# The ends of the FFN blocks of a one-layer encoder step: another order of loads, weights and normalization

## The chip, the cores and the metric

The kernel runs on one core of one Trainium2 chip. The metric is the device time of one execution in microseconds (us), lower is better. The core has the engines PE (TensorE, matrix products), DVE (VectorE), ACT (ScalarE), POOL (GpSimd) and SP (SyncE, which here issues DMAs). A tile framework takes the operations as the program writes them, gives them buffers ("slots" of named tags) and semaphores, and may put instructions of one engine into another order than written.

## What is computed

One layer for 2176 tokens (17 tiles of 128). A mixer (attention, delta rule, state space model) comes first and is not touched. Then:

```python
x = layer_norm(DN_ALPHA * x + mix, lp['ln1_g'], lp['ln1_b'])
hid = jnp.square(jax.nn.relu(x @ lp['w_up'] + lp['b_up']))            # 1024 -> 4096
x = layer_norm(DN_ALPHA * x + hid @ lp['w_down'], lp['ln2_g'], lp['ln2_b'])   # 4096 -> 1024
```

`layer_norm` takes mean and variance over the 1024 features of a token, divides by the square root of variance + 1e-5, multiplies by g and adds b.

## The kernel before

Every matrix product is made of three: each operand is split into a rounded high part (an ACT cast to fp32r) and the rest (a subtraction, on DVE or POOL), and `mm3` sums high x high, low x high and high x low in PSUM. Rows of PE with L68, L69, L70 are these three.

The FFN (from about 1436 us on) goes over three blocks of tokens, 6, 6 and 5 tiles (`BLOCKS`), and in a block over 16 chunks `c` of 256 of the 4096 hidden features. For one chunk there is first the up product, in a Strassen-like form with seven products instead of eight: `f_up1` makes four (operands B11, T2, T3, T1) and `f_up2` three (B21, T4, B22). `f_up_raw` loads the chunk's weights (tile `wur`, two DMAs of 512 KB), `f_up_weights` makes seven combinations and splits them: seven ACT casts and eleven POOL operations of 128x512 into seven slots `wu`. `f_up2` ends with relu, square and the split of the result into `hh` and `hl` (`f_h`). Then the down product: `f_down_weights` loads two halves (`wdr`, three slots) and splits them into `wdh`, `wdl` (two slots each); `f_down` goes tile by tile, half by half of the 1024 outputs, with 2 x 3 matmuls each (12 for a tile, four PSUM slots `fdp`), and a DVE sum adds each result to `fy`, which holds y of the block's tiles (L1583 in chunk 0, L1585 otherwise).

In the steady state PE's order is: three products of `f_up2(c)`, four of `f_up1(c+1)`, then `f_down(c)`; the weights are made one chunk ahead.

At the end of blocks 0 and 1 three things meet. The next block's x must be loaded and transformed (`f_load`, per tile: a load into a `wdr` slot, eight PE transposes into PSUM tiles `ftps`, two ACT copies into `fxs`, four POOL subtractions, seven ACT casts and seven DVE subtractions): it is written between the tiles of `f_down(14)`, as only then the operands `fx...` of the block are free. The hidden part of chunk 15, whose `f_up2` is written with the argument `down`, is split only behind `f_down(14)`. And y of each tile is normalized as soon as it is summed up (`layer_norm` on DVE, `norm`, `later`), stored to the output `o_y`, and only then its `fy` slot can take the next block's x. Chunk 0 of the next block needs its weights again, which `f_up_raw(0)` and `f_up_weights` make anew.

In the last block the products of chunks 14 and 15 are summed in one `f_down`, and each tile is normalized after its sums: four tiles with ACT and POOL (`light`), the last with DVE.

SP issues all DMAs in one queue in program order, and a DMA that waits for a slot holds up what is behind it. Places that the prediction names: `f_load` L1406 to L1437, `f_down` L1569 to L1586, `norm` and `later` L1601 to L1607, the block ends L1639 to L1658, `layer_norm` L1296 to L1317, `rsqrt` L349 to L351.

Of the kernel before, what the change touches and what calls it, by code (L numbers as in the profile page):

```python
# [39 lines left out]

LOADS = 5
LATE = 1


class K:
# [31 lines left out]
    def run(self, upto=99):  # L77
        nc, A = self.nc, self.A
        with self.es:
# [22 lines left out]
            self.x1 = d.tile([NT, DM], F32, name="x1")  # L102
            self.ident = self.ld(self.cst, "c_ident")
# [1192 lines left out]
    def layer_norm(self, pool, y, g, b, tag, light=None):  # L1296


        nc = self.nc
        V = nc.vector  # L1300
        bs = pool.tile([128, 2, nc.vector.BN_STATS_DIM], F32, name=tag + "bs", tag=tag + "bs")
        for i in range(2):
            V.bn_stats(bs[:, i], y[:, i * 512:(i + 1) * 512])
        mv = pool.tile([128, nc.vector.BN_AGGR_DIM], F32, name=tag + "mv", tag=tag + "mv")
        V.bn_aggr(mv, bs)
        ve = pool.tile([128, 1], F32, name=tag + "ve", tag=tag + "ve")
        V.tensor_scalar(ve, mv[:, 1:2], 1e-5, None, OP.add)
        rn = self.rsqrt(pool, ve, 1, tag)
        if light:
            nm = pool.tile([128, 1], F32, name=tag + "nm", tag=tag + "nm")  # L1310
            V.scalar_tensor_tensor(nm, mv[:, 0:1], -1.0, rn, OP.mult, OP.mult)
            nc.scalar.activation(y, y, AF.Identity, scale=rn, bias=nm)
            light.tensor_tensor(y, y, g, OP.mult)
            light.tensor_tensor(y, y, b, OP.add)
            return
        V.scalar_tensor_tensor(y, y, mv[:, 0:1], g, OP.subtract, OP.mult)
        V.scalar_tensor_tensor(y, y, rn, b, OP.mult, OP.add)  # L1317
# [21 lines left out]
    def w_out(self, es):  # L1339
# [9 lines left out]
        for t in range(1, NTILE + 1):  # L1349
# [7 lines left out]
            if t in (6, 8, 10, 12, 14, 16):  # L1357
                self.f_load(0, t // 2 - 3, self.fx0, rp, "mr", 2)
# [26 lines left out]
    def w_norm(self, t, y, pool, g, b):  # L1385
        y = y.rearrange("p k t -> p (k t)")
        self.layer_norm(pool, y, g, b, "l1")
        self.nc.sync.dma_start(self.x1[t * 128:(t + 1) * 128], y)
# [15 lines left out]
    def f_load(self, t0, i, ops, pool, tag, bufs):  # L1404


        nc = self.nc
        x = pool.tile([128, DM], F32, name="fxr", tag=tag, bufs=bufs)
        nc.sync.dma_start(x, self.x1[(t0 + i) * 128:(t0 + i + 1) * 128])
        xs = [self.fx.tile([128, 4, 128], F32, name="fxs", tag=f"fxs{j}") for j in range(2)]  # L1410
# [8 lines left out]
        c1, c2 = (self.fx.tile([128, 4, 64], F32, name=n, tag=n) for n in ("fxc1", "fxc2"))  # L1419
        P = nc.gpsimd  # L1420

        def split(o, src):
            ts = slice(i * 64, i * 64 + 64)
            self.split(ops[o][0][:, :, ts], ops[o][1][:, :, ts], src)

        split("B11", b["B11"])
        P.tensor_tensor(c1, b["B12"], b["B11"], OP.subtract)  # L1427
        P.tensor_tensor(c2, b["B22"], c1, OP.subtract)
        split("T2", c2)
        P.tensor_tensor(b["B12"], b["B22"], b["B12"], OP.subtract)  # L1430
        split("T3", b["B12"])
        split("T1", c1)
        split("B21", b["B21"])
        P.tensor_tensor(c2, b["B21"], c2, OP.subtract)
        split("T4", c2)
        split("B22", b["B22"])
# [69 lines left out]
    def f_up2(self, s, h, down=None):  # L1506
# [5 lines left out]
        def relu2(r, i, src):  # L1512
# [3 lines left out]
        def keep(r, i, q):  # L1516
# [4 lines left out]

        def done(r, i, q, src):
            relu2(r, i, src)
            keep(r, i, q)
# [7 lines left out]
        if down:  # L1532
            for ps, o in (("x", "B21"), ("z", "T4"), ("v", "B22")):
                self.f_product(s, ps, o, False)
            relu2(c22, 1, c22)
            c21, c12 = add("z"), add("v")
            relu2(u, 0, s["x"])
            relu2(c21, 1, c21)
            relu2(c12, 0, c12)
            down()  # L1540
            keep(u, 0, 0)
            keep(c12, 0, 1)
            keep(c21, 1, 0)
            keep(c22, 1, 1)
            return
# [23 lines left out]
    def f_down(self, c, h, wd, ys):  # L1569
# [5 lines left out]
        for i, y in enumerate(ys):  # L1575
            ts = slice(i * 128, (i + 1) * 128)
            for z in range(2):
                zs = slice(z * 512, (z + 1) * 512)
                ps = self.fdp.tile([128, 512], F32, name="fdp", tag="fd")
                for k in range(m):  # L1580
                    self.mm3(ps, h[k][0][:, ts], h[k][1][:, ts], wd[k][0][:, zs], wd[k][1][:, zs], k == 0, k == m - 1)
                if c == 0:
                    V.scalar_tensor_tensor(y[:, zs], y[:, zs], ALPHA, ps, OP.mult, OP.add)  # L1583
                else:
                    V.tensor_tensor(y[:, zs], y[:, zs], ps, OP.add)  # L1585
            yield i  # L1586

    def ffn(self, es):
# [10 lines left out]
        norms = []  # L1599

        def norm(t, y, light):  # L1601
            self.layer_norm(self.fe, y, *rows, "l2", light)
            nc.sync.dma_start(A["o_y"][t * 128:(t + 1) * 128], y)

        def later(n):
            for _ in range(min(n, len(norms))):
                norm(*norms.pop(0))  # L1607

        def run(steps):
            for _ in steps:  # L1610
                pass

        for bi, (t0, nt) in enumerate(BLOCKS):
# [3 lines left out]
            for c in range(NC):  # L1617
                if bi + c == 0:
                    w = self.wu0
# [3 lines left out]
                later(2)  # L1623
                if c:
                    wd = self.f_down_weights(c - 1)
                if c < NC - 1:
                    if c:
                        run(self.f_down(c - 1, h, wd, ys))
                    h = self.f_h(nt)
                    self.f_up2(s, h)  # L1630
                    later(2)
# [7 lines left out]
            h15 = self.f_h(nt) if not last else None  # L1639
            if not last:  # L1640
                t1, n1 = BLOCKS[bi + 1]

                def down():
                    nonlocal ops
                    ops = self.f_x(n1)
                    for i in self.f_down(NC - 2, h, wd, ys):
                        if i < LOADS:
                            self.f_load(t1, i, ops, self.fw, "wdr", 3)

                self.f_up2(s, h15, down)  # L1650
                wd = self.f_down_weights(NC - 1)
                w = self.f_up_weights(self.f_up_raw(0))
                for i in self.f_down(NC - 1, h15, wd, ys):
                    if i + LOADS < n1:
                        self.f_load(t1, i + LOADS, ops, self.fw, "wdr", 3)
                    norms.append((t0 + i, ys[i], nc.vector))
                    if i >= LATE:
                        later(1)  # L1658
            else:
# [7 lines left out]
                for i in self.f_down(NC - 2, h + h15, wd, ys):  # L1667
                    norm(t0 + i, ys[i], nc.gpsimd if i < nt - 1 else None)
# [117 lines left out]
```

## Time and profile before

| | |
|---|---|
| time, median of 3 runs (lowest, highest) | 2952.27 us (2949.34, 2952.82) |
| the profiled execution: time, span | 2949.45 us, 2947.7 us |
| mean granted TensorE clock of it | 0.981 |
| PE busy | 2803.6 us, 95% of the span |
| DVE, ACT, POOL busy | 1996.0, 1324.7, 930.5 us (68, 45, 32%) |
| chain that ended last | PE 71%, DVE 15%, DMA 4%, ACT 3%, issue 3%, POOL 3% |

Busy time is the time in which an engine executes; the span is the time from the first to the last instruction of the profiled execution. The chain is followed back from the last instruction to what released it each time, so its shares tell which engine was the last to be waited for. The shares are means over very different stages; for a change at certain places the rows of these places count.

### The profile page before, as it was taken

What the parts mean: (1) busy time and instruction counts of PE and PEld (TensorE: products, weight loads), DVE (VectorE), ACT (ScalarE), POOL (GpSimd) and SP (SyncE); (2) the same over time, 40 slices, a digit from 0 to 9 for tenths busy, and PEclk for the clock granted to TensorE, in tenths of its full rate; (3) what the DMA queues carried; (4) which work ended last, traced back from release to release, by engine and by line L of the source; (5) the groups of instructions that cost most, each with busy time, mean ns of one, the idle gap of its engine ahead of it and who ended that gap; (6) DMA issues with size and microseconds to landing.
All of it is one profiled execution on the core that took longest, in us unless ns stands there. A gap on an engine that the chain in (4) does not pass through costs nothing.

```text
span 2947.7 us, 46191 instructions
## 1 busy us (share of the span) xinstructions
PE 2803.6 (95%) x16677; PEld 2451.0 (83%) x16677; DVE 1996.0 (68%) x5093; ACT 1324.7 (45%) x2735; POOL 930.5 (32%) x842
## 2 busy tenths in 40 slices
PE   8999999989999999999999999988999998899996
PEld 8988888867777777788889899967999897799996
DVE  7588887797655778778755555497555557855557
ACT  3554544342456666612334344453334345444442
POOL 0011111231100000002554544554544445555653
PEclk9999999989999999999999999999999999999998
DMA  5634454464557441144512122133112122422221
GB/s 183 199 106 127 108 138 112 131 174 122 179 195 224 141 129 51 58 168 165 185 66 86 57 67 77 58 118 122 61 63 81 58 72 95 144 76 73 86 86 43
DMA packets 282923, 330.37 MB, mean 112 GB/s; under 512 B 84530, under 2 KB 217478, under 8 KB 282374
## 3 DMA queue, kind: packets, MB, share of 16 engines
q1 hardware_dynamic: 282694, 327.42, 35.5%
q8 instruction: 131, 2.15, 0.3%
q14 instruction: 98, 0.80, 0.1%
HBM read 265.04 MB, written 64.93 MB: 112 GB/s over the span
## 4 chain that ended last, share of the span: by engine, by line
PE 71%; DVE 15%; DMA 4%; ACT 3%; issue 3%; POOL 3%; SPq 0%; ACTq 0%; POOLq 0%; DVEq 0%
PE fdp L68 7%; PE fdp L69 7%; PE fdp L70 7%; PE pps L69 3%; PE pps L70 3%; PE pps L68 3%; PE aob L1220 2%; PE fupx L69 2%; PE fupx L68 2%; PE fupx L70 2%; PE wops L69 2%; PE wops L68 2%; PE wops L70 2%; PE fupz L70 2%; PE fupz L68 2%
## 5 line engine op out<-in xcount | busy, mean ns | idle before, releaser
L1459 POOL TENSOR_TENSOR wu<-wur,wu 128x512 fp32r<-128x512 f32 x329 | 444.5, 1356 | 683.1 <-ACT wu L1458 672.7
L1585 DVE TENSOR_TENSOR fy<-fy,fdp 128x512 f32<-128x512 f32 x500 | 342.3, 687 | 306.2 <-PE fdp L70 306.0
L68 PE MATMUL fdp<-wdh,hh 128*128 128x512 f32 x1068 | 419.8, 395 | 21.6 <-DVE fy L1583 12.2
L70 PE MATMUL fdp<-wdh,hl 128*128 128x512 f32 x1068 | 418.1, 392 | 1.1 <-DVE hl L1520 1.1
L69 PE MATMUL fdp<-wdl,hh 128*128 128x512 f32 x1068 | 418.7, 392 | 0.0
L1458 ACT CAST wu<-wur 128x512 fp32r<-128x512 f32 x329 | 202.9, 619 | 421.3 <-DMA wur<-in_w_upL 165.1
L68 PE MATMUL pps<-xh,wh 128*128 128x384 f32 (+2 forms) x800 | 280.5, 352 | 9.0 <-ACT xh L63 8.6
L69 PE MATMUL pps<-xl,wh 128*128 128x384 f32 (+2 forms) x800 | 279.5, 350 | 2.9 <-DVE xl L64 2.8
L70 PE MATMUL pps<-xh,wl 128*128 128x384 f32 (+2 forms) x800 | 277.5, 347 | 0.5 <-DVE wl L64 0.3
L68 PEld LDWEIGHTS fdp<-wdh,hh 128*128 128x128 f32 x1068 | 202.2, 190 | 66.0 <-DVE fy L1583 13.8
L70 PEld LDWEIGHTS fdp<-wdh,hl 128*128 128x128 f32 x1068 | 202.1, 189 | 44.3 <-DVE hl L1520 1.9
L69 PEld LDWEIGHTS fdp<-wdl,hh 128*128 128x128 f32 x1068 | 202.1, 189 | 40.2
L63 ACT CAST wdh<-wdr 128x1024 fp32r<-128x1024 f32 x94 | 98.1, 1049 | 262.9 <-PE fdp L70 262.9
L1520 DVE TENSOR_TENSOR hl<-fre,hh 128x384 fp32r<-128x384 f32 (+1 forms) x186 | 137.7, 743 | 71.5 <-ACT hh L1519 71.5
L68 PEld LDWEIGHTS pps<-xh,wh 128*128 128x128 f32 x800 | 152.2, 191 | 19.7 <-ACT xh L63 9.1
L69 PEld LDWEIGHTS pps<-xl,wh 128*128 128x128 f32 x800 | 152.2, 190 | 14.3 <-DVE xl L64 5.4
L70 PEld LDWEIGHTS pps<-xh,wl 128*128 128x128 f32 x800 | 151.9, 190 | 11.3 <-issue 1.8
L64 DVE TENSOR_TENSOR wl<-wr,wh 128x512 fp32r<-128x512 f32 (+1 forms) x152 | 105.3, 699 | 61.1 <-ACT wh L63 57.9
L63 ACT CAST wh<-wr 128x512 fp32r<-128x512 f32 (+1 forms) x152 | 92.8, 619 | 78.2 <-DMA wr<-in_w_inA 39.7
L64 DVE TENSOR_TENSOR wdl<-wdr,wdh 128x1024 fp32r<-128x1024 f32 x94 | 116.1, 1237 | 3.1 <-ACT wdh L63 3.1
L1427 POOL TENSOR_TENSOR fxc<-fxs 128x256 f32<-128x256 f32 x17 | 20.8, 1223 | 294.8 <-ACT fxs L1417 288.8
L1189 ACT ACTIVATE P<-P,st 128x640 f32<-128x640 f32 (+4 forms) x128 | 97.2, 761 | 35.5 <-DVE st L1186 35.3
(555 smaller groups left out, 7289.9 us busy)
## 6 DMA issues: line engine op xcount, KB each, us to landing
wur<-in_w_upL SPq DMA_DIRECT2D x96, 512.0 KB
wdr<-in_w_dnL SPq DMA_DIRECT2D x96, 512.0 KB
wr<-in_w_inA SPq DMA_DIRECT2D x70, 512.0 KB
TU<-tD SPq DMA_DIRECT2D x34, 256.0 KB
y<-in_x SPq DMA_DIRECT2D x17, 512.0 KB
x<-y SPq DMA_DIRECT2D x17, 512.0 KB
fxr<-x SPq DMA_DIRECT2D x17, 512.0 KB
fy<-x SPq DMA_DIRECT2D x17, 512.0 KB
```

The lines of the kernel that those rows point to most:

```text
L63: nc.scalar.copy(hi, src)
L64: nc.vector.tensor_tensor(lo, src, hi.bitcast(F32), OP.subtract)
L68: mm(out, lh, rh, start=first, stop=False, **kw)
L69: mm(out, lh, rl, start=False, stop=False, **kw)
L70: mm(out, ll, rh, start=False, stop=last, **kw)
L1189: nc.scalar.activation(x, x, AF.Exp, scale=-1.0, bias=st[:, q:q + 1], accum_out=st[:, 2 + q:3 + q])
L1220: mm(ob[q * 64:q * 64 + 64, p], vt[j][:, h * 64:(h + 1) * 64], PT[:, k], start=j == 0, stop=j == nk - 1)
L1427: P.tensor_tensor(c1, b["B12"], b["B11"], OP.subtract)
L1458: self.nc.scalar.copy(hi, src)
L1459: P.tensor_tensor(lo, src, hi.bitcast(F32), OP.subtract)
L1520: V.tensor_tensor(hl, r, hh.bitcast(F32), OP.subtract)
L1585: V.tensor_tensor(y[:, zs], y[:, zs], ps, OP.add)
```

## The change

The values computed are the same. There are five parts:

1. `f_load` becomes a generator with three steps: the DMA; the transposes, copies, POOL subtractions and casts to the high parts; the low parts (five on DVE, two on POOL). At a block end `step(k)` after tile k of `f_down(14)` and `f_down(15)` starts the next load at k = 0, 1, 3, 5, 7, 9.
2. The last two tiles of `f_down(14)` and the first two of `f_down(15)` are made as a pair, with the half of the weights as the outer loop and four PSUM tiles at a time. The hidden part of chunk 15 lies in four of the seven `wu` slots, and `f_up2` is the usual one.
3. The weights of chunk 0 are stored to DRAM (`wu0D`, seven DMAs of 512 KB) at the start of the FFN and read back at the block ends, three while `f_down(15)` runs and four behind it.
4. y of blocks 0 and 1 goes unnormalized to DRAM (`x2`) and is normalized in the next block, one tile in every second chunk (`norm_left`): loaded behind `f_up1` of an odd chunk, and in the next chunk its statistics after tile 0 of `f_down`, the square root after tile 1, the product with ACT and POOL after tile 2.
5. `layer_norm` works in halves of 512 columns, and `rsqrt1` makes the inverse root of ten TENSOR_SCALAR operations, on 128x1. In the last block three tiles go by ACT and POOL and two by DVE, and the last tile is stored in halves.

```diff
-LOADS = 5
-LATE = 1
+LOADS = (0, 1, 3, 5, 7, 9)
...
+    def rsqrt1(self, pool, var, eps, tag, pin):
...
+        pin(V.tensor_scalar(x, var, eps, None, OP.add))
+        y = y.bitcast(I32)
+        V.tensor_scalar(y, x.bitcast(I32), 1, None, OP.logical_shift_right)
+        V.tensor_scalar(y, y, -1.0, float(0x5f3759df), OP.mult, OP.add)
+        V.tensor_scalar(xh, x, -0.5, None, OP.mult)
+        cur = y.bitcast(F32)
+        for _ in range(3):
+            V.tensor_scalar(s, cur, cur, xh, OP.mult, OP.mult)
+            V.tensor_scalar(z, s, 1.5, cur, OP.add, OP.mult)
+            cur = z
+        return z
...
+        for o in ("B11", "B21", "B22", "T1", "T2", "T4", "T3"):
+            nc.scalar.copy(self.f_part(ops, o, 0, i), b[o])
+        yield
+        for o in ("B11", "B21", "B22", "T1", "T2", "T4", "T3"):
+            e = P if o in ("B21", "B22") else nc.vector
+            e.tensor_tensor(self.f_part(ops, o, 1, i), b[o], self.f_part(ops, o, 0, i).bitcast(F32), OP.subtract)
...
+    def f_up_again(self, i):
+
+        w = self.fw.tile([128, 2, 4, 128], F32R, name="wu", tag="wu", bufs=7)
+        self.nc.sync.dma_start(w.rearrange("p a b c -> p (a b c)").bitcast(F32), self.wu0D[i])
+        return w
...
+            todo = [(i + j, z) for j in range(2 if i == pair else 1) for z in range(2)]
...
+            for x, k in [(x, k) for k in range(m) for x in todo] if ps else [(x, k) for x in todo for k in range(m)]:
...
+        def norm_left():
+            t = left.pop(0)
+            ts = slice(t * 128, (t + 1) * 128)
+            y = [self.fx.tile([128, 512], F32, name="fyn", tag=f"fxs{j}") for j in range(2)]
+            for j in range(2):
+                nc.sync.dma_start(y[j], self.x2[ts, j * 512:j * 512 + 512])
+            yield
+            yield from self.layer_norm(self.fe, y, *rows, "l2", nc.gpsimd,
...
-                self.f_up2(s, h15, down)
+                self.f_up2(s, h15)
+                ops = self.f_x(n1)
+                loads = [self.f_load(t1, i, ops, self.fw, "wdr", 3) for i in range(n1)]
...
+                for i in self.f_down(NC - 2, h, wd, ys, nt - 2):
+                    step(i)
                 wd = self.f_down_weights(NC - 1)
-                w = self.f_up_weights(self.f_up_raw(0))
-                for i in self.f_down(NC - 1, h15, wd, ys):
-                    if i + LOADS < n1:
-                        self.f_load(t1, i + LOADS, ops, self.fw, "wdr", 3)
-                    norms.append((t0 + i, ys[i], nc.vector))
-                    if i >= LATE:
-                        later(1)
+                w = []
+                for i in self.f_down(NC - 1, h15, wd, ys, 0):
+                    t = t0 + i
+                    nc.sync.dma_start(self.x2[t * 128:(t + 1) * 128], ys[i])
+                    left.append(t)
+                    step(nt + i)
+                    if 1 <= i <= 3:
+                        w.append(self.f_up_again(i - 1))
+                w = iter(w + [self.f_up_again(i) for i in range(3, 7)])
...
-                    norm(t0 + i, ys[i], nc.gpsimd if i < nt - 1 else None)
+                    norm(t0 + i, ys[i], nc.gpsimd if i < nt - 2 else None, i == nt - 1)
```

How the order of instructions changes is shown at two places, both at the end of block 0. The first is PE's queue where the down product of chunk 14 ends and that of chunk 15 begins; `ftps` rows are transposes of a loaded tile, and `hh` and `h15h` are high parts of the hidden features. Before:

```order
L1416 MATMUL ftps<-ld_c_ident,fxr 128x128 [waits DMAHW6_49,Activation_49]
L1416 MATMUL ftps<-ld_c_ident,fxr 128x128 x3
L1416 MATMUL ftps<-ld_c_ident,fxr 128x128 [waits Activation_49]
L1416 MATMUL ftps<-ld_c_ident,fxr 128x128 x3
L68 MATMUL fdp<-wdh,hh_20977 128x512 [waits DVE_49,Activation_49]
L68 MATMUL fdp<-wdh,hh_20977 128x512 [waits DVE_49] x3
L68 MATMUL fupx<-fxB11h,wu 128x384 [waits Activation_49]
L69 MATMUL fdp<-wdl,hh_20977 128x512 [waits DVE_49]
L70 MATMUL fdp<-wdh,hl_20978 128x512
```

And of the change:

```order
L1442 MATMUL ftps<-ld_c_ident,fxr 128x128 [waits DMAHW3_49,PE_49]
L1442 MATMUL ftps<-ld_c_ident,fxr 128x128 x3
L1442 MATMUL ftps<-ld_c_ident,fxr 128x128 [waits Activation_49]
L1442 MATMUL ftps<-ld_c_ident,fxr 128x128 x3
L66 MATMUL fdp<-wdh,h15h_20892 128x512 [waits Activation_49]
L66 MATMUL fdp<-wdh,h15h_20892 128x512 x3
L1442 MATMUL ftps<-ld_c_ident,fxr 128x128 [waits DMAHW6_49,PE_49]
L1442 MATMUL ftps<-ld_c_ident,fxr 128x128 x2
L67 MATMUL fdp<-wdl,h15h_20892 128x512 [waits DVE_49]
L68 MATMUL fdp<-wdh,h15l_20893 128x512
```

Before, the first four matmuls of chunk 15 are high parts only, and a matmul of the next block's up product stands among them. Now the transposes of two tile loads stand around the four high parts of the second half of chunk 15's weights, and the low parts come behind them.

The second place is SP's queue there. `wur` are raw up weights, `wdr` down weights, `fxr` x of a tile to be transformed, `x_89` the x after the mixer, `x_90` the new DRAM tile for y, and `wu0D` the stored weights. Before:

```order
L1442 DMA wur<-in_w_upL 128x1024 [waits DMAHW7_49,DMAHW6_49,Pool_49]
L1442 DMA wur<-in_w_upL 128x1024 [waits DMAHW1_49]
L1409 DMA fxr<-x_89 128x1024 [waits PE_49]
L1409 DMA fxr<-x_89 128x1024 [waits DMAHW4_49,PE_49]
L1560 DMA wdr<-in_w_dnL 128x1024 [waits DMAHW5_49,PE_49]
L1560 DMA wdr<-in_w_dnL 128x1024 [waits DMAHW2_49,PE_49]
L1409 DMA fxr<-x_89 128x1024 [waits DMAHW3_49,PE_49]
L1560 DMA wdr<-in_w_dnL 128x1024 [waits DMAHW6_49,PE_49]
L1560 DMA wdr<-in_w_dnL 128x1024 [waits DMAHW4_49,DMAHW0_49,DVE_49]
L1560 DMA wdr<-in_w_dnL 128x1024 [waits DMAHW5_49,DMAHW1_49,DVE_49]
L1603 DMA out_o_y<-fy_17293 128x1024 [waits DVE_49]
L1560 DMA wdr<-in_w_dnL 128x1024 [waits DMAHW7_49,DVE_49]
```

And of the change:

```order
L1501 DMA wu<-wu0D 128x1024 [waits PE_49]
L1501 DMA wu<-wu0D 128x1024 [waits DMAHW0_49,PE_49]
L1501 DMA wu<-wu0D 128x1024 [waits PE_49]
L1434 DMA fxr<-x_89 128x1024 [waits PE_49]
L1434 DMA fxr<-x_89 128x1024 [waits DMAHW3_49,PE_49]
L1569 DMA wdr<-in_w_dnL 128x1024 [waits DMAHW4_49,PE_49]
L1569 DMA wdr<-in_w_dnL 128x1024 [waits DMAHW5_49,DMAHW4_49,DVE_49]
L1434 DMA fxr<-x_89 128x1024 [waits DMAHW6_49,DMAHW2_49,PE_49]
L1569 DMA wdr<-in_w_dnL 128x1024 [waits DMAHW7_49,DMAHW3_49,PE_49]
L1569 DMA wdr<-in_w_dnL 128x1024 [waits DMAHW5_49,DMAHW0_49,DVE_49]
L1702 DMA x_90<-fy_17206 128x1024 [waits DMAHW1_49,DVE_49]
L1702 DMA x_90<-fy_17208 128x1024 [waits DVE_49]
```

The two loads of raw weights for the next block's chunk 0 have gone; three loads of finished weights stand in their place, four more follow later, and stores of unnormalized y into `x_90` stand where the normalized outputs were.

## Rows read from the trace of the kernel before

**Rows 1.** The profile page's first line

```profile
span 2947.7 us, 46191 instructions
```

**Rows 2.** Busy time by stretch: stretch, its length, each engine's busy time (instructions), PEclk, DMA

```profile
1500.00:1900.00 400.00, 400.00 (x2005) 363.98 (x2004) 211.01 (x296) 161.45 (x284) 181.77 (x141) 1.00 0.21 68
1908.61:2034.18 125.57, 102.08 (x482) 86.91 (x481) 110.46 (x223) 61.67 (x122) 62.59 (x52) 0.92 0.37 125
2445.62:2567.76 122.14, 105.14 (x521) 88.94 (x521) 110.24 (x224) 60.59 (x120) 68.12 (x56) 0.96 0.34 121
2897.21:2947.70 50.49, 27.99 (x122) 22.19 (x120) 40.82 (x99) 6.95 (x9) 19.84 (x8) 0.82 0.13 52
```

**Rows 3.** Waits of PE at the end of block 0 (1908.61 to 2034.18)

```profile
PE fdp L68 <- DVE fy L1583: 8.4, 1, 8.4
...
PE fdp L68 <- DVE hl L1520: 6.4, 1, 6.4
```

**Rows 4.** Timeline of PE in steady state: start, duration, engine, line, operation

```profile
1606.97 0.34 PE L68 MATMUL fupx<-fxB21h,wu 128*128 128x384 f32 x1
...
1621.81 0.39 PE L68 MATMUL fdp<-wdh,hh 128*128 128x512 f32 x1
...
1638.13 0.34 PE L68 MATMUL fupx<-fxB21h,wu 128*128 128x384 f32 x1
...
1911.33 1.04 PE L1416 MATMUL ftps<-ld_c_ident,fxr 128*128 128x128 f32 x8
...
2619.74 0.31 PE L68 MATMUL fupx<-fxB21h,wu 128*128 128x320 f32 x1
...
2632.06 0.40 PE L68 MATMUL fdp<-wdh,hh 128*128 128x512 f32 x1
```

**Rows 5.** Timeline of DVE, two tile loads in a row

```profile
1927.51 0.96 DVE L64 TENSOR_TENSOR fxT1l<-fxc,fxT1h 128x256 fp32r<-128x256 f32 x1
...
1932.49 0.96 DVE L64 TENSOR_TENSOR fxT1l<-fxc,fxT1h 128x256 fp32r<-128x256 f32 x1
```

**Rows 6.** Timelines of ACT, DVE and SP at the end of block 0

```profile
1941.65 1.04 ACT L63 CAST wdh<-wdr 128x1024 fp32r<-128x1024 f32 x1
...
1943.60 1.21 DVE L64 TENSOR_TENSOR wdl<-wdr,wdh 128x1024 fp32r<-128x1024 f32 x1
...
2003.87 0.34 SPq L1603 DMA_DIRECT2D out_o_y<-fy  x1
...
2006.52 0.32 SPq L1635 DMA_DIRECT2D fy<-x  x1
```

**Rows 7.** Timelines of SP and POOL at the start of the FFN

```profile
1444.56 0.81 SPq L1442 DMA_DIRECT2D wur<-in_w_upL  x2
...
1447.81 0.33 SPq L1388 DMA_DIRECT2D x<-y  x1
...
1449.03 2.56 POOL L1459 TENSOR_TENSOR wu<-wur,wu 128x512 fp32r<-128x512 f32 x2 [4.50 <-ACT wu L1458]
```

**Rows 8.** Timelines of POOL and PE in a chunk of block 2

```profile
2648.80 3.15 POOL L1459 TENSOR_TENSOR wu<-wur,wu 128x512 fp32r<-128x512 f32 x2 [4.33 <-ACT wu L1458]
...
2654.53 0.31 PE L68 MATMUL fupz<-fxT3h,wu 128*128 128x320 f32 x1
```

**Rows 9.** Timelines of PE, POOL and DVE in the tail

```profile
2918.29 2.40 POOL L1313 TENSOR_TENSOR fy<-fy,row_ln_g 128x1024 f32<-128x1024 f32 x1 [3.73 <-ACT fy L1312]
...
2918.72 0.15 DVE L344 TENSOR_SCALAR l2t<-l2ve 128x1 int32<-128x1 int32 x1
...
2919.10 1.61 DVE L349 TENSOR_TENSOR l2s<-l2y 128x1 f32<-128x1 f32 x1
...
2924.80 0.40 PE L70 MATMUL fdp<-fxT1h,fxT2l 128*128 128x512 f32 x1
...
2933.94 0.68 DVE L1585 TENSOR_TENSOR fy<-fy,fdp 128x512 f32<-128x512 f32 x1
...
2942.66 1.28 DVE L1317 SCALAR_TENSOR_TENSOR fy<-fy,l2z,row_ln_b 128x1024 f32<-128x1024 f32 x1
```

More of the change, by code (lines that the diff above doesn't have):

```diff
@@ L1293, in a_sample, with layer_norm @@
             V.tensor_copy(self.sos[rr, :, bs], ob[rr, :, q * 16:q * 16 + 16])
-    def layer_norm(self, pool, y, g, b, tag, light=None):
+    def rsqrt1(self, pool, var, eps, tag, pin):
+        V = self.nc.vector
+        t = pool.tile([128, 5], F32, name=tag + "r", tag=tag + "r")
+        x, xh, s, z, y = (t[:, i:i + 1] for i in range(5))
+        pin(V.tensor_scalar(x, var, eps, None, OP.add))
[9 more added lines that the diff above has]
+        return z
+    def layer_norm(self, pool, y, g, b, tag, light=None, store=None, pin=lambda i: i):
         nc = self.nc
@@ L1357, in w_out @@
             if t in (6, 8, 10, 12, 14, 16):
-                self.f_load(0, t // 2 - 3, self.fx0, rp, "mr", 2)
+                for _ in self.f_load(0, t // 2 - 3, self.fx0, rp, "mr", 2):
+                    pass
             if t == 14:
@@ L1386, in w_norm @@
         y = y.rearrange("p k t -> p (k t)")
-        self.layer_norm(pool, y, g, b, "l1")
+        for _ in self.layer_norm(pool, [y[:, 0:512], y[:, 512:1024]], g, b, "l1"):
+            pass
         self.nc.sync.dma_start(self.x1[t * 128:(t + 1) * 128], y)
@@ L1531, in f_up2 @@
         c22 = s["c22"]
[L1532 to L1545, printed above, removed]
         done(c22, 1, 1, c22)
@@ L1567, in f_down_weights, with f_down @@
         return out
-    def f_down(self, c, h, wd, ys):
+    def f_down(self, c, h, wd, ys, pair=None):
         nc = self.nc
@@ L1598, in ffn, with norm, store @@
         rows = None
[L1599 to L1610, printed above, removed]
-                pass
+        left, late = [], None
+        def norm(t, y, light, halves=False):
+            def store(i):
+                hs = slice(i * 512, i * 512 + 512)
+                if halves:
+                    nc.sync.dma_start(A["o_y"][t * 128:(t + 1) * 128, hs], y[:, hs])
+                elif i:
+                    nc.sync.dma_start(A["o_y"][t * 128:(t + 1) * 128], y)
+            for _ in self.layer_norm(self.fe, [y[:, 0:512], y[:, 512:1024]], *rows, "l2", light, store):
+                pass
+        def norm_left():
[4 more added lines that the diff above has]
+                nc.sync.dma_start(y[j], self.x2[ts, j * 512:j * 512 + 512])
+            yield
+            yield from self.layer_norm(self.fe, y, *rows, "l2", nc.gpsimd,
+                                       lambda j: nc.sync.dma_start(A["o_y"][ts, j * 512:j * 512 + 512], y[j]),
+                                       self.tc.keep_in_program_order)
         for bi, (t0, nt) in enumerate(BLOCKS):
@@ L1622, in ffn @@
                 s = self.f_up1(c, ops, nt, w)
-                later(2)
+                if left and c % 2 == 1:
+                    late = norm_left()
+                    next(late)
                 if c:
@@ L1627, in ffn @@
                     if c:
-                        run(self.f_down(c - 1, h, wd, ys))
+                        for i in self.f_down(c - 1, h, wd, ys):
+                            if late and c % 2 == 0:
+                                next(late, None)
+                        if c % 2 == 0:
+                            late = None
                     h = self.f_h(nt)
                     self.f_up2(s, h)
-                    later(2)
                 if c == 0:
```

117 lines of the change are left out of this document (64 added, 53 removed).

## The prediction

> **What bounds the kernel now.** I read the page's first parts, then busy time by stretches, then PE's waits at the block ends, then single rows. The span of the profiled execution is 2947.7 us [rows 1]; its own time is 2949.45, so 1.75 lies around the span, and the median shown, 2952.27, is 2.8 above it. In the middle of block 0 PE is busy for 400.00 of 400 us at a granted clock of 1.00, with DVE at 211, ACT at 161, POOL at 182 [rows 2]: nothing that only relieves another engine there can pay. Losses are to be had in three stretches alone: the end of block 0 (PE 102.08 of 125.57, clock 0.92, DVE 110.46), the end of block 1 (105.14 of 122.14, clock 0.96, DVE 110.24) and the tail (27.99 of 50.49, DVE 40.82) [rows 2]. In the first two DVE is the engine that PE waits for; the longest waits are 8.4 us for the first sum of the new block, whose `fy` must be normalized, stored and reloaded first, and 6.4 for the split of the hidden part of chunk 15 [rows 3].
>
> **What a block end would take without waits.** Seven products of 6 tiles take 1621.81 - 1606.97 = 14.84 us, a down product of 6 tiles 1638.13 - 1621.81 = 16.32 (72 matmuls, 0.227 each, 2.72 a tile), seven products of 5 tiles 2632.06 - 2619.74 = 12.32, and a down product of 5 tiles by count 60/72 x 16.32 = 13.60; eight transposes take 1.04 [rows 4]. The first stretch holds three down products, 18 up products and 6 x 8 transposes: 3 x 16.32 + 18/7 x 14.84 + 6 x 1.04 = 93.4, against 125.57 [rows 2], a loss of 32.2. The second holds two down products of 6 tiles, two of 5, 18 products and 5 x 8 transposes: 32.6 + 27.2 + 31.7 + 5.2 = 96.7 against 122.14, a loss of 25.4. Together 57.6. Of this some (1 - 0.92) x 125.57 = 10 and (1 - 0.96) x 122.14 = 5 is the lower clock, which these two rows show where PE idles and the full stretch does not; the rest is waits.
>
> **Part 1 and 2, loads and the pair.** Before, DVE does a tile load in 1932.49 - 1927.51 = 4.98 us [rows 5], written between tiles of 2.72 us, so DVE falls behind, and all that is DVE's in the block end (sums, splits, normalization) with it. Now a load comes every two tiles, 2 x 2.72 + 1.04 = 6.5 us, with two of seven subtractions on POOL. That removes DVE as the bound. Of each load the same transposes, copies, casts and one DMA are issued, only later. What is late next are the halves of the weights for `f_down(15)`: the second half's load waits for a `wdr` slot that DVE frees with the first half's low part. From a free slot it takes the transfer (2.65 us from the issue of a 512 KB store to that of the load that waited for it, 2006.52 - 2003.87), the cast 1.04 and the subtraction 1.21 [rows 6]: 4.90. PE has twelve matmuls, 2.72, and eight transposes, 1.04, to cover it: 1.14 are missing, and with the queueing at the slot I take 2 for each of two halves. Bounds: 0, if the queued loads arrive early, and 6.4 each, the wait of today [rows 3]. The change of four PSUM tiles at once costs 0.7 (one 512-column sum of 0.68 [rows 9] before the first slot is free; bounds 0 and 1.4, two sums). The clock costs 15 us over 42.6 us of waits today, 0.4 for each us of wait, so 4.7 us of waits cost 1.8 more. New loss 6.5 per end, 13 for both; the gain is 57.6 - 13 = 44.6.
>
> **Part 3, weights read back.** At each block end seven casts and eleven POOL operations go, seven loads of 512 KB come. The four late ones are issued when `f_down(15)` has ended, one behind the other on SP; each lands 2.65 us after its start [rows 6] if alone, some 6 if two or three share the DMA engines (an estimate from the same row). The fourth product needs its slot three products later, 3 x 14.84/7 = 6.4. So 0, with a bound of 3 us in all if SP, whose queue they share with stores of y, is late. What hides them is PE's first three products; without these each us late is a us lost. At the FFN start seven stores join SP's queue, and the second load of raw weights for chunk 1 now comes behind the last store of x, 1447.81 instead of 1444.56 [rows 7]. POOL's chain that waits for it starts at 1449.03 [rows 7], and PE waits for that chain. I take 1 us; bounds -0.5 (nothing, and a store less in the way) and 4 (the full shift of 3.25 and one DMA issue).
>
> **Part 4, late normalization.** DVE's two statistics, the ten small steps and two ACT passes fall in full stretches where DVE has half its time free [rows 2]. The place to fear is POOL: four operations of 128x512, 1.3 each (half of the 2.56 for two [rows 7]), 5.2 in one go, in front of the weights' low parts in POOL's queue. In block 2 POOL idles 4.33 us just there, and the low part that comes at 2648.80, done by 2650.4, is used by the third product at 2654.53 [rows 8]. So a shift of 0.9 meets 4.1 of slack: 0. The instruction that may wait is POOL's first multiplication, for ACT's pass; behind it are all low parts of the weights, and PE waits for these. Bounds 0 and 12 x 0.9 = 11.
>
> **Part 5, the tail.** PE's last matmul starts at 2924.80 and takes 0.40, but the sum that uses it only at 2933.94, 8.7 late, and the last DVE instruction ends at 2942.66 + 1.28 = 2943.94 [rows 9]. DVE is late because TENSOR_TENSOR of 128x1 takes 1.61 us beside a POOL pass of 2.40 us (row POOL 2918.29), where a TENSOR_SCALAR of 128x1 in the same pass takes 0.15 [rows 9]. The new inverse root is all TENSOR_SCALAR, so DVE keeps up. Behind the last matmul's end at 2925.2 stand the sum 0.68, its statistics (as long, by estimate), the fourth tile's second pass 1.28, the fifth's first pass 1.28, ten small steps at 0.2 (0.15 and the gap), and the second pass 1.28: 7.2, so 2932.4, against 2943.94. That is 11.5; the sums beside POOL's passes of the third tile take back about 1: 10.5. Bounds 7 and 11.5.
>
> The Trainium skill, page "SBUF — State Buffer", section "Who interferes with whom", says that a DVE instruction with two SBUF inputs contends with a GpSimd instruction that reads SBUF; the 1.61 us agrees. It also says that `tensor_scalar` can enter two-port modes and contend; the 0.15 us beside the 2.40 us pass does not show it for 128x1. If it held here, the small steps would wait as before, and the tail would give 7 rather than 10.5.
>
> **The sum.** 44.6 + 10.5 - 1 = 54.1. From the profiled 2949.45 that is 2895.3; the median shown is 2.8 higher, and with some of that I predict 2897.
>
> **Rivals.**
> A, as summed: 2897, own range 2889 to 2908. For it: PE's row of the full stretch shows that it can run without any wait when its inputs are early.
> B, the wait for the weights of `f_down(15)` takes the place of the one removed: both halves 6.4 instead of 2 at both ends, 4 x 4.4 = 17.6 more waits, with the clock's 0.4 for each 24.6: 2921. For it: one set of three `wdr` slots now serves loads of x and weights in turn. Against it: the 4.90 worked out above.
> C, the waits go wholly: 13 more, less what the clock still shows, 2885. For it: the high parts of the second half are used first, and DVE's low part is hidden by them. Against it: the slot order on SP.
> D, the read-back weights are late: SP's queue holds them behind stores of y that wait for sums; 3 to 4 us at each end with the clock, 2905.
> E, slower: POOL's four normalization passes, with the first waiting for ACT, hold up the weights' low parts in every even chunk. It begins where a tile holds POOL for more than 4.33 + 4.1 = 8.4 us (5.2 is its own work) and each us beyond costs 12, as there are 12 tiles; to end slower than before, at 2960, the hold must be some 13.6 us. The statistics, the root and the pass come after different tiles of `f_down`, 2.72 us apart, and are short, which speaks against it.
> F, the change does not do what it says, as the order keeps the waits (DVE's queue has the loads' low parts ahead of the sums): 2940 to 2952. Against it: PE's queue has the transposes and the high parts apart.
>
> **Chances.** A 0.60, B 0.16, C 0.11, D 0.06, E 0.04, F 0.03. The predicted time is A's. The range reaches to C below, and to B above: 2882 to 2924. About 0.2%, 6 us, is what a measurement can tell from no change: faster takes A to D and half of F, 0.93 in all with rounding against me, the same 0.03, slower 0.04.
>
> **What would show it.** PE busy over 95% in the two block ends, clock above 0.97 there; no wait for `fy` or `hl` of several us, but one or two of about 2 us for `wdh` or `wdl`; the DVE row of the last sum within 1 us of the last matmul's end, and small TENSOR_SCALARs at 0.15 us beside POOL; POOL's idle gap in even chunks of block 2 filled and no PE wait for `wu`. It is wrong if PE shows waits for `wu` in the new block, or waits in even chunks only, or if the block ends lose over 12 us each.

## The result and the profile after

The changed kernel takes 2915.5 us (2911.07 to 2917.92) against 2950.81; the ratio is 0.9879, interval 0.9862 to 0.9896. Forecast were 2897 and a range of 2882 to 2924: faster, inside the range, but with some 35 us gained where 54 were summed up.

Busy time by stretches of the changed kernel, the same four stretches as in [rows 2] (in this order: length, then PE, its weight loads, DVE, ACT and POOL with their instructions, then the granted clock, the DMA share and GB/s):

```profile
1500.00:1900.00 400.00, 400.00 (x2001) 363.57 (x2000) 210.61 (x297) 158.42 (x279) 181.19 (x141) 1.00 0.21 69
1918.29:2018.93 100.64, 93.91 (x481) 83.14 (x481) 63.75 (x95) 51.02 (x108) 61.27 (x60) 1.00 0.50 181
2430.37:2535.33 104.96, 98.63 (x521) 85.22 (x521) 67.75 (x112) 50.14 (x106) 66.45 (x61) 1.00 0.45 163
2873.43:2913.20 39.77, 28.01 (x122) 22.17 (x120) 30.81 (x89) 6.55 (x11) 16.34 (x12) 0.89 0.17 66
```

The block ends went from 125.57 to 100.64 and from 122.14 to 104.96, the tail from 50.49 to 39.77. DVE is down from 110 to 64 and 68 us there, and the granted clock is 1.00 instead of 0.92 and 0.96: PE's own busy time for the same matmuls is 8.2 and 6.5 us less, about the 10 and 5 that the prediction read as the lower clock. What PE still waits for at the end of block 0, against [rows 3]:

```profile
PE fupv L66 <- DMA wu<-wu0D: 1.8, 1, 1.8
PE fdp L66 <- ACT wdh L61: 1.5, 1, 1.5
PE fdp L67 <- DVE wdl L62: 1.4, 1, 1.4
PE fdp L66 <- ACT fxs L1443: 1.0, 1, 1.0
PE fdp L66 <- DVE fy L1600: 1.0, 1, 1.0
```

Two of the five are the halves of chunk 15's down weights. They come about as ACT's and DVE's timelines show:

```profile
1946.91 1.04 ACT L61 CAST wdh<-wdr 128x1024 fp32r<-128x1024 f32 x1 [1.26 <-DMA wdr<-in_w_dnL]
```

```profile
1940.09 1.27 DVE L1600 TENSOR_TENSOR fy<-fy,fdp 128x512 f32<-128x512 f32 x2
1941.28 1.45 DVE L62 TENSOR_TENSOR wdl<-wdr,wdh 128x1024 fp32r<-128x1024 f32 x1
```

The first half's low part stands behind two sums on DVE; the second half's load takes some 4.2 us from the slot that this low part frees (1942.73) to its cast (1946.91). One wait is new and lies in the steady part of block 2 (PE's waits from 2560 to 2870):

```profile
PE fupz L68 <- POOL wu L1482: 7.3, 5, 1.7
```

The whole of the two profiled executions, cut at the same matmuls of PE's order (us):

| stage | before | after | difference |
|---|---|---|---|
| before the FFN (to its first up matmul) | 1436.07 | 1443.74 | +7.7 |
| FFN start, chunks 0 and 1 | 77.42 | 79.42 | +2.0 |
| rest of block 0, up to chunk 15 | 388.76 | 388.76 | 0 |
| end of block 0 | 117.09 | 92.17 | -24.9 |
| rest of block 1 | 419.92 | 419.92 | 0 |
| end of block 1, to chunk 2 | 128.51 | 111.32 | -17.2 |
| rest of block 2, up to chunk 14 | 311.84 | 320.49 | +8.7 |
| last products | 45.59 | 45.62 | 0 |
| behind the last matmul | 22.47 | 11.81 | -10.7 |
| span | 2947.67 | 2913.25 | -34.4 |

Up to the `w_out` stage both kernels have the same instructions in the same order, so the 7.7 us in front need a cause of their own.

### The profile page after: what moved, and what is told of

The parts are those of the page before. It is cut to its first block, busy times and chain, and to the rows that moved or that the text cites. A ratio compares the mean times of both kernels' runs of the same rounds, so it can differ in the third digit from the quotient of the medians.

```text
span 2913.2 us, 46312 instructions
## 1 busy us (share of the span) xinstructions
PE 2795.9 (96%) x16677; PEld 2447.0 (84%) x16677; DVE 1963.9 (67%) x4972; ACT 1319.0 (45%) x2735; POOL 1001.0 (34%) x906
## 4 chain that ended last, share of the span: by engine, by line
PE 47%; POOL 6%; DMA 3%; DVE 2%; ACT 2%; issue 1%; SPq 0%; DVEq 0%; ACTq 0%; POOLq 0%
PE fdp L67 7%; PE fdp L68 7%; PE fdp L66 7%; POOL wu L1482 2%; DMA wur<-in_w_upL 2%; PE wops L66 2%; PE wops L67 2%; PE wops L68 2%; PE fupz L68 2%; PE fupv L66 2%; PE fupv L68 2%; PE fupv L67 2%; PE fupz L66 2%; PE fupz L67 2%; PE fupx L66 2%; PE fupx L67 2%
## 5 line engine op out<-in xcount | busy, mean ns | idle before, releaser
L1482 POOL TENSOR_TENSOR wu<-wur,wu 128x512 fp32r<-128x512 f32 x315 | 420.3, 1338 | 556.7 <-ACT wu L1481 544.3
L66 PE MATMUL fdp<-wdh,hh 128*128 128x512 f32 x1020 | 397.7, 390 | 2.0 <-DVE fy L1600 1.9
L68 PE MATMUL fdp<-wdh,hl 128*128 128x512 f32 x1020 | 397.1, 389 | 0.0
L67 PE MATMUL fdp<-wdl,hh 128*128 128x512 f32 x1020 | 397.1, 389 | 0.0
L66 PEld LDWEIGHTS fdp<-wdh,hh 128*128 128x128 f32 x1020 | 191.4, 188 | 41.7 <-DVE fy L1600 3.7
L68 PEld LDWEIGHTS fdp<-wdh,hl 128*128 128x128 f32 x1020 | 191.5, 188 | 40.3 <-DVE hl L1547 0.2
L67 PEld LDWEIGHTS fdp<-wdl,hh 128*128 128x128 f32 x1020 | 191.5, 188 | 37.9 <-DVE wdl L62 0.2
L1547 DVE TENSOR_TENSOR hl<-fre,hh 128x384 fp32r<-128x384 f32 (+1 forms) x180 | 155.4, 864 | 89.8 <-ACT hh L1546 88.1
L68 PEld LDWEIGHTS pps<-xh,wl 128*128 128x128 f32 x800 | 151.8, 190 | 11.7 <-issue 1.8
L62 DVE TENSOR_TENSOR wdl<-wdr,wdh 128x1024 fp32r<-128x1024 f32 x94 | 133.4, 1421 | 15.7 <-ACT wdh L61 15.7
L1542 ACT ACTIVATE fre<-fre,ld_b_up 128x384 f32<-128x384 f32 (+1 forms) x144 | 85.9, 597 | 74.3 <-DVE fre L1551 48.4
```

The costliest lines, as they stand in the source:

```text
L62: nc.vector.tensor_tensor(lo, src, hi.bitcast(F32), OP.subtract)
L66: mm(out, lh, rh, start=first, stop=False, **kw)
L67: mm(out, lh, rl, start=False, stop=False, **kw)
L68: mm(out, ll, rh, start=False, stop=last, **kw)
L1482: P.tensor_tensor(lo, src, hi.bitcast(F32), OP.subtract)
L1547: V.tensor_tensor(hl, r, hh.bitcast(F32), OP.subtract)
```

## The experiments

The times of different experiments come from several chips, so they are compared by the ratio to the kernel before, which was timed beside each. Stages are compared between single profiled executions.

**Two more looks at the unchanged kernels.** Both kernels again, with no edit.

> The kernel before, unchanged, for a second look at its attention stage (914 to 1256 us), which took 342.1 us in its first trace, 350.5 in the changed kernel's and 341.1 to 348.1 in the four experiments so far, with the same instructions in the same order. Theory 1 (the granted clock there falls in a pattern that differs from execution to execution): the stage differs by some us from 342.1, and the granted clock of its parts with it. Theory 2 (something in the changed program makes it slower): again 342 within 0.5 us and the same clock part by part.

> The changed kernel, unchanged, beside the others on this chip. Theory 1 (the clock in the attention stage varies between executions): that stage is not 350.5 us again but somewhere between 341 and 351; all stages behind it as in the first trace within 0.3 us. Theory 2 (the changed program makes it slower): 350 within 0.5 us. The ratio to before again 0.986 to 0.990.

Measured: 2960.76 us for the one run of before; 2918.33 for the changed kernel, ratio 0.9883 (0.9865 to 0.9901). The attention stage by busy time, in the first look at before, the first at after, the second at before, the second at after (the column before the last two is the granted clock):

```profile
914.44:1256.49 342.05, 320.65 (x2665) 251.81 (x2664) 260.91 (x832) 222.18 (x499) 9.24 (x27) 0.95 0.36 112
```

```profile
913.72:1264.16 350.44, 328.43 (x2665) 259.16 (x2664) 261.25 (x832) 222.14 (x499) 9.18 (x27) 0.93 0.35 110
```

```profile
918.03:1268.35 350.32, 329.52 (x2666) 260.50 (x2664) 261.17 (x832) 222.23 (x499) 9.20 (x27) 0.92 0.36 110
```

```profile
917.58:1258.75 341.17, 318.98 (x2665) 251.63 (x2664) 261.06 (x832) 222.01 (x499) 9.39 (x27) 0.95 0.37 113
```

The two kernels have changed places: 342 and 350 belong to executions, not to programs, and the longer stage has the lower clock at the same count of instructions. So the +7.7 is no effect of the change. What sets the pattern of the clock in one execution is open. Of the second look's other stages three missed the 0.3 us that were expected: the FFN start took 0.4 less, the end of block 1 0.9 more, the rest of block 2 1.2 more. So a stage difference of about 1 us between two single executions is no evidence by itself.

**The late normalization of block 2 on DVE.**

```diff
-            yield from self.layer_norm(self.fe, y, *rows, "l2", nc.gpsimd,
+            yield from self.layer_norm(self.fe, y, *rows, "l2", None if last else nc.gpsimd,
```

> The changed kernel, but in block 2 the late normalization is applied by DVE (four SCALAR_TENSOR_TENSOR of 128x512) in place of ACT and POOL; block 1 as changed. Theory 1 (POOL's four passes, begun late and two of them at 2.27 us, push the low parts of the weights past the third product): the waits of PE for wu in block 2, five of up to 1.7 us, 7.3 in all, vanish, block 2 gets about 8.6 us shorter, the time is about 2907. Theory 2 (the statistics and the root on DVE, or the loads of y, are what comes late): PE still waits in the even chunks, and the time stays within 2 us of 2915. Theory 3 (DVE's passes of 0.7 us each delay DVE's sums and the splits of the hidden part): new waits for fy or hl, time not below 2915.

Measured: 2907.83, ratio 0.9838 (0.9825 to 0.9851). The stretch from chunk 3 up to chunk 13 of block 2, ten chunks, in the changed kernel and then in the experiment:

```profile
2561.29:2829.86 268.57, 261.20 (x1441) 235.77 (x1440) 180.64 (x280) 123.79 (x232) 191.13 (x131) 1.00 0.29 97
```

```profile
2562.74:2822.34 259.60, 259.60 (x1441) 235.85 (x1440) 181.25 (x295) 117.95 (x221) 160.07 (x112) 1.00 0.30 100
```

With 31 us less on POOL, PE is busy in all of its 259.60 us: 9.0 gained, theory 1. In the changed kernel POOL's timeline, and PE's, around one late normalization show how:

```profile
2586.00 1.30 POOL L1482 TENSOR_TENSOR wu<-wur,wu 128x512 fp32r<-128x512 f32 x1 [0.73 <-ACT wu L1481]
2587.38 1.30 POOL L1494 TENSOR_TENSOR wur<-wur 128x512 f32<-128x512 f32 x1
2588.64 2.27 POOL L1333 TENSOR_TENSOR fyn<-fyn,row_ln_g 128x512 f32<-128x512 f32 x1
2590.98 1.42 POOL L1334 TENSOR_TENSOR fyn<-fyn,row_ln_b 128x512 f32<-128x512 f32 x1
2592.37 2.27 POOL L1333 TENSOR_TENSOR fyn<-fyn,row_ln_g 128x512 f32<-128x512 f32 x1
2594.71 1.42 POOL L1334 TENSOR_TENSOR fyn<-fyn,row_ln_b 128x512 f32<-128x512 f32 x1
2596.11 3.03 POOL L1482 TENSOR_TENSOR wu<-wur,wu 128x512 fp32r<-128x512 f32 x2
```

```profile
2597.68 0.42 PE L68 MATMUL fupz<-fxT3h,wu 128*128 128x320 f32 x1 [1.17 <-POOL wu L1482]
```

Two things differ from the kernel before, in the chunk of [rows 8], whose first up matmul and whose first use of the low part by the third product are

```profile
2645.72 0.31 PE L68 MATMUL fupx<-fxB21h,wu 128*128 128x320 f32 x1
...
2654.82 0.31 PE L70 MATMUL fupz<-fxT3h,wu 128*128 128x320 f32 x1
```

The four passes take 7.5 us (2588.64 to 2596.11), not 5.2, since two of them run at 2.27. And POOL reaches them late: its chain for the weights ends 1.4 us behind the chunk's first up matmul (2588.68 and 2587.25), where before it ended 1.3 ahead of it (2648.80 - 4.33 and 2645.72). The third product's low part comes just 1.2 us too late for PE. The slow passes stand beside DVE's subtractions, which are slow as well (DVE's timeline):

```profile
2589.68 1.57 DVE L1547 TENSOR_TENSOR hl<-fre,hh 128x320 fp32r<-128x320 f32 x1
2591.18 2.31 DVE L62 TENSOR_TENSOR wdl<-wdr,wdh 128x1024 fp32r<-128x1024 f32 x1
```

The second took 1.21 in [rows 6]. The Trainium skill, page "SBUF — State Buffer", section "Who interferes with whom", has a DVE instruction with two SBUF inputs contend with a GpSimd instruction that reads SBUF; both sides of it are in these rows. The other traces agree: in block 1 of the changed kernel the four passes stand elsewhere in the chunk and take 1.29 each (2029.60 to 2034.88 for the first tile), and over the ten chunks above the subtractions of 128x1024 take 1.88 us in the mean in the changed kernel, 1.57 without POOL's passes, and 1.22 in the kernel before.

**The root alone.** The kernel before with the new inverse root and nothing else.

```diff
...
-        rn = self.rsqrt(pool, ve, 1, tag)
...
+        for _ in range(3):
+            V.tensor_scalar(s, rn, rn, xh, OP.mult, OP.mult)
+            V.tensor_scalar(z, s, 1.5, rn, OP.add, OP.mult)
+            rn = z
```

> The kernel before with one thing of the change alone: the inverse root of ten TENSOR_SCALAR operations (layer_norm whole, nothing else changed). Theory 1 (at the block ends the bound was DVE's loads of x and the order of the work, the root matters in the tail alone): tail about 8 us shorter, because the 128x1 operations no longer wait for POOL's passes; block ends within 3 us each of before; time about 2942. Theory 2 (the waits of the small operations beside POOL also made the block ends late, 12 normalizations stand there): each block end some 8 us shorter as well, time about 2927. Theory 3 (TENSOR_SCALAR waits for POOL's passes too): nothing changes, 2949 to 2951.

Measured: 2930.89, ratio 0.9917 (0.9902 to 0.9932). Behind the last matmul 11.7 us instead of 22.5, as short as in the changed kernel (11.8), so the halves and the other split of the last tiles show no gain beyond that of the root. The first block end with all of block 1's rest is 530.2 instead of 537.0, the second with block 2's rest 438.4 instead of 440.4: 6.8 and 1.9 won, so neither 3 each nor 8 each. With 0.6 at the start these are 20 us, half of the 42 that the FFN stages of the whole change gained. What is left of PE's waits at the end of block 0 with the root alone:

```profile
PE fdp L68 <- DVE hl L1528: 6.4, 1, 6.4
PE ftps L1424 <- ACT fxs L1425: 3.6, 5, 1.4
PE fdp L68 <- DVE fy L1591: 2.5, 3, 1.1
```

Of the 8.4 for `fy` of [rows 3] 2.5 are left, in three waits; the 6.4 for `hl` has stayed, and that one the new order of the work removes. From chunk 15 to chunk 2 of block 1, DVE's operations of 128x1 took 26.8 us in sum before, 23.3 of them in 60 TENSOR_TENSOR and SCALAR_TENSOR_TENSOR; with the root alone they take 13.2, all as TENSOR_SCALAR.

**The old root in the tail.** The changed kernel with `rsqrt` in the last block's `norm` only.

```diff
-        rn = self.rsqrt1(pool, mv[:, 1:2], 1e-5, tag, pin)
+        if tail:
...
+            rn = self.rsqrt(pool, ve, 1, tag)
+        else:
+            rn = self.rsqrt1(pool, mv[:, 1:2], 1e-5, tag, pin)
```

> The changed kernel with the old inverse root (TENSOR_TENSOR and SCALAR_TENSOR_TENSOR on 128x1) in the last block's normalization alone, so only the tail changes. Theory 1 (the small operations waited for POOL's passes, and that made the tail late): from the last matmul's end to the end of the span 18 to 20 us instead of 11.8, and rows of 128x1 of over 1 us. Theory 2 (the other split of the last tiles, two on DVE, does it): within 2 us of 11.8.

Measured: 18.4 us behind the last matmul instead of 11.8, theory 1. Two of DVE's rows shortly before, and the two passes of POOL beside them:

```profile
2888.99 1.26 DVE L350 TENSOR_TENSOR l2s<-l2s,l2h 128x1 f32<-128x1 f32 x1
2890.35 1.14 DVE L351 SCALAR_TENSOR_TENSOR l2z<-l2s,l2y 128x1 f32<-128x1 f32 x1
```

```profile
2888.94 1.29 POOL L1339 TENSOR_TENSOR fy<-fy,row_ln_b 128x512 f32<-128x512 f32 x1
2890.19 1.29 POOL L1338 TENSOR_TENSOR fy<-fy,row_ln_g 128x512 f32<-128x512 f32 x1
```

Each of the two small operations ends with its pass, at 2890.25 and 2891.49 (the passes at 2890.23 and 2891.48). In the changed kernel a TENSOR_SCALAR lies wholly inside a pass and takes 0.14:

```profile
2898.44 0.14 DVE L1303 TENSOR_SCALAR l2r<-l2r 128x1 int32<-128x1 int32 x1
```

```profile
2897.88 1.79 POOL L1334 TENSOR_TENSOR fy<-fy,row_ln_b 128x512 f32<-128x512 f32 x1
```

Yet its time is 2915.48, ratio 0.9875 (0.9856 to 0.9893), no slower: each chunk of blocks 0 and 1 took 30.95 us instead of 31.16. That is taken up below.

**No pair.**

```diff
-                for i in self.f_down(NC - 2, h, wd, ys, nt - 2):
+                for i in self.f_down(NC - 2, h, wd, ys):
-                for i in self.f_down(NC - 1, h15, wd, ys, 0):
+                for i in self.f_down(NC - 1, h15, wd, ys):
```

> The changed kernel without the pair: all tiles of the down products of chunks 14 and 15 one by one, both halves of the weights in each. Theory 1 (the pair gives the halves of chunk 15's weights the time of twelve matmuls to be swapped): at each block end both halves are split only behind the last tile, PE waits 5 to 6 us there instead of 2.8, the time rises by 5 to 8 us, to some 2922. Theory 2 (the pair only moves the wait): within 2 us of the changed kernel.

Measured: 2923.63, ratio 0.9888 (0.9874 to 0.9903), which the interval does not part from the changed kernel's 0.9883. The stages do at one end: the second block end is 5.5 longer, theory 1; the first 0.9, no more than two looks at one kernel differ. PE's longest waits in the two, where with the pair the wait for `wdh` was 1.5 and 1.3:

```profile
PE fdp L66 <- ACT wdh L61: 3.7, 2, 2.1
...
PE fdp L66 <- ACT wdh L61: 4.7, 2, 3.2
```

**Weights made anew.** No stores of `wu0`, and `w = self.f_up_weights(self.f_up_raw(0))` ahead of `f_down(15)` at the block ends.

> The changed kernel without the stored weights: no stores at the start of the FFN, and at both block ends the weights of chunk 0 are loaded raw and made anew (seven casts, eleven POOL operations) as before the change. Theory 1 (the stores cost the start about 2 us, the read-back saves little as POOL has room): start of the FFN 2 us shorter, block ends 0 to 3 us longer each, in all within 4 us of the changed kernel. Theory 2 (POOL's eleven operations, 14 us, collide with POOL's part of the loads of x, and four combinations can begin only when the down product of chunk 15 has ended): PE waits for wu at the start of each next block, 5 to 10 us each, time 2923 to 2933.

Measured: 2925.50, ratio 0.9897 (0.9882 to 0.9912). Start 2.5 us shorter, block ends 8.2 and 7.6 longer, the rest of block 2 5.2 longer: theory 2. In the profiled execution, the slowest of the four, that is some 18 us for reading back, net of the stores; the prediction priced only the read-back's lateness (0) and gave it no share of the gain. The times moved less, by the ratios some 4 us of 2950, and their intervals overlap; how much of the 18 an average execution shows is open.

**Three edits together.** The normalization edit above; the raw second half of chunk 15's down weights in a free `wu` slot; the last y stored behind the late read-backs.

```diff
+            if wu and k:
+                wr = self.fw.tile([128, 1024], F32, name="wdr", tag="wu", bufs=7)
...
-                    nc.sync.dma_start(self.x2[t * 128:(t + 1) * 128], ys[i])
+                    if i < nt - 1:
+                        nc.sync.dma_start(self.x2[t * 128:(t + 1) * 128], ys[i])
...
                 w = iter(w + [self.f_up_again(i) for i in range(3, 7)])
+                nc.sync.dma_start(self.x2[t * 128:(t + 1) * 128], ys[nt - 1])
```

> The changed kernel with three edits: the late normalization of block 2 applied by DVE; the raw second half of chunk 15's down weights loaded into a free slot of the up weights instead of the slot that the first half's split must free; the store of the last tile's y issued behind the four late loads of stored weights. Theory 1 (the waits at the block ends are those slots and that queue): the wait for the second half's wdh (1.5 and 1.3 us) and the wait for a stored weight at the end of block 0 (1.8) go, some 4 us less than with the normalization edit alone, ratio to before about 0.982. Theory 2 (other waits take their place, as ACT and DVE are busy with loads there): the time stays within 1.5 us of the normalization edit alone, ratio 0.9838.

Measured: 2897.45, ratio 0.9815 (0.9798 to 0.9833): faster than both kernels. At the end of block 0 there is left of the waits shown for the changed kernel:

```profile
PE fdp L66 <- DVE fy L1603: 1.9, 2, 1.0
PE fdp L67 <- DVE wdl L62: 1.2, 1, 1.2
PE fupv L66 <- DMA wu<-wu0D: 0.2, 1, 0.2
```

The wait for the second `wdh` and most of that for `wu0D` have gone, theory 1; the block ends are 1.8 and 4.5 us shorter than with the normalization edit alone.

**A shift in SBUF.** The three edits with unused tiles in front of the FFN's other pools, six or one.

```diff
+        for i in range(6):
+            self.fe.tile([128, 1], F32, name=f"pad{i}", tag=f"pad{i}")
         self.fh = self.pool("fh", 1, es=es)
```

> The kernel with the three edits and nothing else than six unused tiles of 128x1 in the FFN's first pool, so that the hidden features, the weights and y lie a little further on in SBUF; the instructions and their order are the same. Asked: why the run with the old root in the tail had a chunk of blocks 0 and 1 in 30.95 us instead of 31.16, each up matmul at 173.7 ns after the other instead of 176.7. Theory 1 (where these tiles lie in SBUF): chunks at 30.95 here too, 6 us less in all, about 2891 beside 2897 for the three edits. Theory 2 (chance between executions, or something else in that kernel): 31.16 again, ratio as with the three edits, 0.9815.

> The same with one unused tile of 128x1 instead of six. Theory 1 (the place in SBUF decides, and any shift may do): either 30.95 or 31.16 for every chunk of blocks 0 and 1, constant over the run, perhaps not the one that six tiles give. Theory 2 (chance): no connection with the tile, 31.16.

Measured: six tiles 2889.51, ratio 0.9785 (0.9766 to 0.9804); one tile 2889.71, 0.9783 (0.9759 to 0.9807). One chunk of block 0 on PE, without and with one tile (first up matmul, first down matmul, next chunk):

```profile
1646.61 0.34 PE L66 MATMUL fupx<-fxB21h,wu 128*128 128x384 f32 x1
...
1661.45 0.39 PE L66 MATMUL fdp<-wdh,hh 128*128 128x512 f32 x1
...
1677.77 0.34 PE L66 MATMUL fupx<-fxB21h,wu 128*128 128x384 f32 x1
```

```profile
1641.33 0.34 PE L66 MATMUL fupx<-fxB21h,wu 128*128 128x384 f32 x1
...
1655.89 0.39 PE L66 MATMUL fdp<-wdh,hh 128*128 128x512 f32 x1
...
1672.26 0.34 PE L66 MATMUL fupx<-fxB21h,wu 128*128 128x384 f32 x1
```

Seven up products take 14.56 us instead of 14.84, the down product the same 16.3. It is so in every full chunk of blocks 0 and 1, so theory 1: the place of the tiles sets the pace, not chance. These two runs were made on another chip than the three edits alone; the run with the old root in the tail was made on the same chip as those and has 30.95 too, so the chip is not the reason. This is the fastest version measured here.

## Why the prediction was right, and where its sum was not

- Block ends: 44.6 us forecast, 24.9 + 17.2 = 42.1 measured. The two waits for the halves of chunk 15's weights were put at 2 us each and are 1.3 to 1.5. They are near by luck in part: the forecast added the second half's load (2.65), cast and low part, but PE's high parts wait for the cast alone, and the load took some 4.2; the first half's wait is DVE's sums ahead of its low part. The wait in the pair, put at 0.7, is 1.0 for a sum of DVE and 1.0 that the trace puts down to a copy of ACT. The clock term, 1.8 per end, did not come: the stretches run at 1.00. Read-back weights, put at 0, cost 1.8 at the end of block 0; in the new block after block 1 PE waits 0.8 twice for weights that POOL makes.
- What the sum put down to the order of the loads could in part be had otherwise: the root alone brings nearly 9 us of the block ends. The prediction read DVE as the bound there, and rightly, but not that part of DVE's time was small operations beside POOL. The two gains can't be added, as in the whole change these normalizations have left the block ends. What the loads in steps, or that move by itself, are worth was not tried.
- Tail: 10.5 forecast, 10.7 measured. That TENSOR_SCALAR of 128x1 does not wait for POOL held; with the old root the tail is 6.6 longer. The last sum starts 1.1 us behind the last matmul's end, where under 1 was named.
- FFN start: 1 us forecast, 2.0 measured, by the step that was named. The second raw load of chunk 1 comes late, and with it the cast that waits for it and POOL's chain; on ACT the first relu stands behind a cast of that chain. PE waits 4.5 us for the relu, before 1.7, and less in other places. ACT's timeline of the changed kernel:

```profile
1459.42 0.62 ACT L1481 CAST wu<-wur 128x512 fp32r<-128x512 f32 x1 [1.88 <-DMA wur<-in_w_upL]
1462.75 0.62 ACT L1481 CAST wu<-wur 128x512 fp32r<-128x512 f32 x1 [2.71 <-POOL wur L1487]
1463.28 0.61 ACT L1542 ACTIVATE fre<-fre,ld_b_up 128x384 f32<-128x384 f32 x1
```

- Late normalization: the step that failed. "So a shift of 0.9 meets 4.1 of slack: 0" was mis-sized by 8.7 us. The passes hold POOL for 7.5 us and not for 5.2, and POOL reaches them some 2.7 us later against PE than in the trace of before. The 4.1 was read at the third product's first matmul; the one that takes the low part stands at 2654.82, and the low part was done by 2650.4, so the slack is 4.4: 2.7 + 7.5 - 4.33 - 4.4 = 1.5, beside 1.2 of wait in this chunk and 1.7 in the longest. The lateness shows in the loads of raw weights, whose one buffer must have been read by POOL first. Before, they are issued 7.8 us behind a chunk's first up matmul from chunk 2 of block 2 on. In the changed kernel block 2 begins late (11.5 in chunk 2); without POOL's passes it begins so too (11.3) but is back between 7.8 and 9.5 from chunk 7 on, while with them the load comes 11.5 to 13.7 behind from chunk 2 to chunk 12. That is rival E's mechanism at about a seventh of its price (8.7 of the 63 us between 2897 and 2960), and it began under the 8.4 us of hold that E named. Block 1, with 31.16 us for a chunk instead of 25.96 and its loads at 8.8 throughout, shows no wait.
- The base: the sum started from an execution of before whose part in front of the FFN took 1436 us, and added 2.8 at the end for the median. That part took 1436 to 1448 in executions of the same program; the sum could not know it, but the range should have allowed for it.
- The signs that the prediction named for being wrong: two of three came, PE's waits for `wu` in the new block and waits in even chunks only. Of those for being right the clock, the waits for `fy` and `hl` and the small TENSOR_SCALARs came as named; PE is busy for 93 and 94% of the two block ends, not over 95, and PE does wait for `wu`.

Taken together, the FFN gained 42.1 us in the first two profiled executions (34.4 + 7.7), of 54.1 forecast; 8.7 of the rest are the normalization in block 2, 2.5 the block ends, 1.0 the start. The times moved by 31 to 41 us (the interval of the ratio); what lies between is taken to be the draw of the stages in front, which is argued from their spread and not shown. By the FFN alone the time would be 2949.45 - 42.1 = 2907, inside A's own range of 2889 to 2908. The median of 2915.5 lies outside that, and inside the stated range only because this was drawn up to rival B, whose 6.4 us of waits for each half did not come. That the number held is luck to this extent.

## What to carry to other kernels

Slack that is read from a trace holds for the queue as it stands there: an operation put ahead of others has to be priced by its duration beside the neighbour it will have, and its start by the buffer that its predecessors wait for. Operations on one column took up to as long as POOL's pass of 512 beside them where they read two tensors, and 0.14 to 0.28 us where they were TENSOR_SCALARs, so look at their neighbours and their form and not at their size. Before a gain of one per cent is traced to its cause, look at the same kernel twice, stage by stage.

## What was not expected of the hardware

An unused tile of one float for each partition, put in front of the FFN's buffers, makes the 128x384 matmuls start 173.4 ns after one another instead of 176.7, while those of 128x512 keep to 227. Six tiles do nearly the same (173.7). Which buffer's place matters, and why, was not tried. The granted clock of the attention stage is 0.92 to 0.95 and its length 341 to 350 us from execution to execution of one program.
